# A hybrid attention and recurrence layer: input split and gate products of the recurrence, order of the keys, figures of the scheduler

## The chip, the cores and the metric

The kernel runs on one NeuronCore of a Trainium2 chip. The metric is the device time of one execution in microseconds; several runs are given by their median. A trace of one further execution was taken by the hardware profiler.

The engines are called TensorE (PE in the rows; PEld is its weight load), VectorE (DVE), ScalarE (ACT), GpSimd (POOL) and SyncE (SP), which issues the DMAs. PSUM, which TensorE writes, has eight banks of 128 partitions by 512 fp32.

## The reference

One encoder layer runs over two sequences, a prompt of 512 tokens and a sample of 1024, both of width 1024 in fp32, with the same weights. The parts that matter here:

```python
n = rms_norm(x, ln1_g) * (1 + sc1) + sh1           # sh, sc, g come from silu(c) @ w_ada
q, k, v, xl, gl = split(n @ w_in)                  # 512 columns each
q, k = rms_norm per head (8 heads of 64)
att = neighbourhood_attention(q, k, v, rpb)        # grid rows of 64 tokens, window of 8 x 16 keys, softmax
xl = depthwise_conv(xl, lru_conv_w, lru_conv_b)    # width 4
for each direction (forward, backward):
    r = sigmoid(blockwise xl @ w_r + b_r)          # 8 blocks of 64 x 64
    i = sigmoid(blockwise xl @ w_i + b_i)
    a = exp(-8 * r * softplus(-lam)); u = sqrt(1 - a*a) * (i * xl)
    h = scan(h = a*h + u)
lru = (h_forward + h_backward) * gelu(gl)
x = x + g1 * (concat(att, lru) @ w_out)
up = depthwise_conv(n2 @ w_up, ...)                # width 3, 2 x 2816 columns
x = x + g2 * ((gelu(up_1) * up_2) @ w_down)
```

## The kernel before

**Matmuls.** Every fp32 product is made of three: an operand is split into a high part (rounded to the type fp32r) and a low part (the rest), and high x high, high x low and low x high are added in PSUM. `split` (line 493) makes the parts: a copy to fp32r, on ScalarE or VectorE, and a subtraction, on VectorE or GpSimd. The large products of the up and down projections use Strassen-Winograd terms, sums and differences of blocks that are split in their turn.

**Stages**, in order of time: modulation vectors and the first norm (to about 44 us); per column block of 128, the projections of queries, keys, values, recurrence input and gate, first for the prompt, then for the sample, woven with the attention of the block before (to about 610 us); output projection and second norm (to about 840 us); up projection, 22 blocks (to about 1440 us); down projection, seven products of 11 pairs of blocks into six banks each (to the end).

**Recurrence, `lru` (line 1005).** After the convolution, `xc` holds 128 channels, two heads of 64, over all tokens of the sequence. Two buffers are made, one for a head: lines 1026 to 1028 split 64 partitions of `xc` so that the high part lies on the head's own partitions and the low part on the other 64. A gate product of 512 tokens and one direction (`mm2_rows`, line 468) is then, for each head, a matmul over all 128 rows, which adds high x high and high x low since the high weights lie on both halves, and one over 64 rows for the low weights. The two 64-row matmuls of the heads lie on different halves of the array's rows. Four sigmoids of 64 partitions empty the two banks.

**Attention, `attend` (line 1070).** A tile has 128 queries and 256 keys (prompt) or 384 (sample): rows of the grid by 32 columns. The scores come from `mm3_rows` (line 451), six matmuls of 64 rows: three pairs, each with one matmul for either head. Their moving operand is read from the keys in the order row, column: runs of 32. VectorE adds the bias and finds the minimum of the negated scores; the exponential (line 1107) reads the tile in order and writes it with four rows innermost, since the values are laid out so; it goes into a second buffer. TensorE transposes the tile, 128 keys at a time, and multiplies it with the values. `qkv` (line 951) stores the keys: line 985 writes the high part out of PSUM, line 986 the low part.

**Order of the work.** The kernel's functions only record operations, with their tiles and an estimated cost. `run` and `_order` (lines 501 and 561) then simulate the five engines once, on the host, and write each engine's instructions in the resulting order; on the chip each engine follows its list. An operation gets a key, the time by which it must be done for its users; of the ready ones the smallest key goes first. Operations other than matmuls that read or write PSUM get `BOOST` ns off their key (line 521). All instructions of the trace therefore carry the line of `_emit` (L359) or `transpose` (L482), and are known by shape and tile.

**Memory.** SBUF is shared between an arena of fp32r tiles (matmul operands, R) and one of fp32 tiles (F). `STEPS` gives the size of R in KB in each stage, out of 216; the rest is F. Pieces (`piece0F`, `piece0R`, ...) change their owner between stages. The sixth entry is that of the down projection, the seventh that of its last product. A tile is placed ahead of its turn only where the memory still suffices for what comes before it.

Of the kernel before, what the change touches and what calls it, by code (L numbers as in the profile page):

```python
# [18 lines left out]
P = 128  # L19
# [12 lines left out]
STEPS = (140, 134, 160, 176, 186, 64, 124)  # L32
# [15 lines left out]
BOOST = 3e5  # L48

LANES = 8  # L50

# [165 lines left out]
class Recorder:  # L217
# [208 lines left out]
    def mm(self, out, lhsT, rhs, start, stop, tile_position=None, also=(), cost=None, go_on=False):  # L426
        n = self._n(rhs)
        if cost is None:
            cost = max(max(64.0, n) / 2.4 + 13.5, 109.0) if rhs.ap.dtype == F32R else max(214.0, n / 0.6)
        kw = dict(out=out, lhsT=lhsT, rhs=rhs, start=start, stop=stop)  # L430
        if tile_position is not None:
            kw["tile_position"] = tile_position
        if go_on:
            kw["skip_group_check"] = True
        w = [out]
        if start:

            w.append(View(out.buf, self._shadow(512, F32), ())[out.span()[0]:out.span()[1], :])
        self.op("PE", cost, self._emit(self.nc.tensor.matmul, kw), [lhsT, rhs], w, also=also)
# [11 lines left out]
    def mm3_rows(self, outs, sts, mvs):  # L451

        n = self._n(mvs[0][0])
        kws = []
        for a, b, start, stop in ((0, 0, True, False), (0, 1, False, False), (1, 0, False, True)):
            for out, st, mv in zip(outs, sts, mvs):
                kws.append(dict(out=out, lhsT=st[a], rhs=mv[b], start=start, stop=stop))
        calls = [self._emit(self.nc.tensor.matmul, kw) for kw in kws]

        def go():  # L460
            for c in calls:
                c()
        w = list(outs)
        for out in outs:
            w.append(View(out.buf, self._shadow(512, F32), ())[out.span()[0]:out.span()[1], :])
        self.op("PE", 3 * (max(64.0, n) / 2.4 + 13.5), go, [v for pr in sts + mvs for v in pr], w)

    def mm2_rows(self, outs, sts, mvs):
# [10 lines left out]
        self.op("PE", 3 * (max(64.0, n) / 2.4 + 13.5), go, [v for pr in sts + mvs for v in pr], list(outs))  # L479
# [21 lines left out]
    def run(self):  # L501
# [5 lines left out]
        for o in ops:  # L507
            if o.eng == "PE":
                vt += o.cost
            o.vt = vt  # L510
            for q in o.deps:
                q.users.append(o)

        for o in reversed(ops):
# [6 lines left out]
            if o.eng != "PE" and not o.strict and any(b.dram is None and b.arena.key == "P" for b in o.bufs):  # L521
                o.key -= BOOST
        base = {}
# [37 lines left out]
    def _order(self, occ):  # L561
# [87 lines left out]
        while count < n:  # L649
# [92 lines left out]
            o.start, o.end = s, s + o.cost  # L742
# [4 lines left out]
            fin = o.end  # L747
# [34 lines left out]
def encoder(ctx: ExitStack, tc: tile.TileContext, x_p, x_s, c_t, ada, bada, bgate, lng, w_qkv, w_xg,  # L782
# [168 lines left out]
    def qkv(q, get, j, out, w, early=False):  # L951
# [3 lines left out]
        for g in range(halves):  # L955
# [29 lines left out]
            R.act(kh[:, c0:c0 + 512], pk, AF.Copy, scale=qkgt[:, 1:2])  # L985
            R.stt(kl[:, c0:c0 + 512], pk, qkgt[:, 1:2], kh[:, c0:c0 + 512].bitcast(F32), ALU.mult, ALU.subtract)
# [18 lines left out]
    def lru(q, get, c, wxg=None, early=False):  # L1005
# [17 lines left out]

        xs = [R.buf([P, nT], F32R, "xcs") for _ in range(2)]
        half = (slice(0, 64), slice(64, P))
        for hd in range(2):
            a, b = half[hd], half[1 - hd]
            R.split(xs[hd][a], xs[hd][b], xc[a])
# [4 lines left out]
        for d in range(2):  # L1033
            for b in blk:
                pg = [R.bank("gate") for _ in range(2)]
                R.mm2_rows(pg, [(gh[:, hd, d, :], gl[half[hd], hd, d, :]) for hd in range(2)], [(x[:, b], x[a, b]) for x, a in zip(xs, half)])
# [33 lines left out]
    def attend(q, j, kqs):  # L1070
# [16 lines left out]
        for grp in groups:  # L1087
            vs = {cb: values(cb) for cb in sorted({cb for _, cb in grp})}
            po = [R.bank("po").rearrange("p (u h d) -> p u h d", u=2, h=2) for _ in range(2)]
            for u, (half, cb) in enumerate(grp):  # L1090
# [5 lines left out]
                for hh in range(2):  # L1096
                    hp = slice(64 * hh, 64 * hh + 64)
                    pS.append(R.bank("S")[:, 0:nk])
                    mvs.append([t[hp, :].rearrange("p (r c) -> p r c", c=64)[:, r0:r0 + nr, KB[cb]:KB[cb] + 32] for t in (kh, kl)])
                    sts.append([x[hp, cb * P:cb * P + P] for x in qs[half]])  # L1100
                R.mm3_rows(pS, sts, mvs)
                for hh in range(2):
                    e, mn, sm, ri = R.buf([P, nk], F32, "e"), small(1, "mn"), small(1, "sm"), small(1, "ri")
                    R.vec("tensor_tensor_reduce", e, [pS[hh], bi[:, hh, :]], in0=pS[hh], in1=bi[:, hh, :], scale=-1.0, scalar=3e38, op0=ALU.add, op1=ALU.min, accum_out=mn)

                    e, raw = R.buf([P, nk], F32, "e"), e
                    R.act(e.rearrange("p (a c r) -> p a r c", c=32, r=4), raw.rearrange("p (a r c) -> p a r c", r=4, c=32), AF.Exp, scale=-1.0, bias=mn, accum_out=sm)
# [467 lines left out]
def _places():  # L1575
# [3 lines left out]
    for rows, halves, knr in ((8, 1, 8), (16, 2, 12)):  # L1579
# [12 lines left out]
        out.append(at.reshape(halves * 4, P, knr * 32))  # L1592
# [72 lines left out]
```

## Time and profile before

| | |
|---|---|
| Runs | 1752.65, 1755.28, 1757.9 us; median 1755.28 us |
| Profiled execution | 1756.22 us, of it the span 1754.4 us |
| TensorE busy | 1683.2 us (96%), 8882 matmuls |
| VectorE busy | 1330.6 us (76%) |
| ScalarE busy | 844.6 us (48%) |
| GpSimd busy | 567.4 us (32%) |
| Mean granted TensorE clock | 0.978 of 2.4 GHz |

The busy time of an engine is the union of its instructions; matmuls overlap, so the mean duration of one says less than the distance between starts. The clock that is granted to TensorE has two levels, 1.2 and 2.4 GHz (0.5 and 1.0 in the rows); a number between is a mean over a stretch.

### The profile page before, as it was taken

What the parts mean: (1) busy time and instruction counts of PE and PEld (TensorE: products, weight loads), DVE (VectorE), ACT (ScalarE), POOL (GpSimd) and SP (SyncE); (2) the same over time, 40 slices, a digit from 0 to 9 for tenths busy, and PEclk for the clock granted to TensorE, in tenths of its full rate; (3) what the DMA queues carried; (4) which work ended last, traced back from release to release, by engine and by line L of the source; (5) the groups of instructions that cost most, each with busy time, mean ns of one, the idle gap of its engine ahead of it and who ended that gap; (6) DMA issues with size and microseconds to landing.
All of it is one profiled execution on the core that took longest, in us unless ns stands there. A gap on an engine that the chain in (4) does not pass through costs nothing. (4 is left out here: it accounts for less than half of the span.)

```text
span 1754.4 us, 24769 instructions
## 1 busy us (share of the span) xinstructions
PE 1683.2 (96%) x8882; PEld 1399.7 (80%) x8882; DVE 1330.6 (76%) x2467; ACT 844.6 (48%) x1444; POOL 567.4 (32%) x353
## 2 busy tenths in 40 slices
PE   6999989999999799998999999999999999998998
PEld 3777687978696588897888888888888787886887
DVE  4788885887878875877777676767677867899785
ACT  3478963868585942364444343434345521232331
POOL 0023130030201210535332222222223402899993
PEclk9999989999999899999999999999999999998999
DMA  9654442252516574552121212121212468577661
GB/s 345 228 180 142 153 137 90 94 204 67 207 52 238 177 243 147 178 195 67 43 85 57 70 57 70 57 71 57 71 62 90 141 236 291 195 274 225 221 213 60
DMA packets 130476, 253.88 MB, mean 145 GB/s; under 512 B 13600, under 2 KB 45984, under 8 KB 130352
## 3 DMA queue, kind: packets, MB, share of 16 engines
q1 hardware_dynamic: 130352, 252.29, 42.5%
q8 instruction: 70, 1.15, 0.3%
q14 instruction: 54, 0.44, 0.1%
HBM read 207.66 MB, written 44.58 MB: 144 GB/s over the span
## 5 line engine op out<-in xcount | busy, mean ns | idle before, releaser
L359 PE MATMUL bank<-arena_r 128*128 128x512 f32 (+2 forms) x2224 | 498.3, 361 | 16.0 <-DVE piece0F L359 7.6
L359 PEld LDWEIGHTS bank<-arena_r 128*128 128x128 f32 (+1 forms) x2224 | 390.2, 192 | 84.4 <-DVE piece0F L359 8.0
L359 PE MATMUL bank<-piece0R,arena_r 128*128 128x512 f32 (+2 forms) x1283 | 353.7, 390 | 1.6 <-DVE arena_s L359 1.6
L359 PE MATMUL bank<-arena_r,piece0R 128*128 128x384 f32 (+3 forms) x1549 | 325.9, 336 | 1.7 <-DVE piece0R L359 1.2
L359 PEld LDWEIGHTS bank<-arena_r,piece0R 128*128 128x128 f32 (+1 forms) x1549 | 254.5, 189 | 28.3 <-issue 12.3
L359 PEld LDWEIGHTS bank<-piece0R,arena_r 128*128 128x128 f32 (+1 forms) x1283 | 230.0, 190 | 57.7 <-issue 12.4
L359 POOL TENSOR_TENSOR arena_f<-arena_f 128x512 f32<-128x512 f32 (+2 forms) x87 | 128.0, 1471 | 354.3 <-DMA arena_f<-in_w_up_dram 157.9
L359 POOL TENSOR_TENSOR arena_r<-arena_f,arena_r 128x512 fp32r<-128x512 f32 (+2 forms) x62 | 97.9, 1583 | 285.0 <-ACT arena_r L359 157.6
L359 ACT ACTIVATE arena_f<-arena_f,arena_s 128x384 f32<-128x384 f32 (+2 forms) x196 | 140.9, 768 | 94.9 <-DVE arena_f L359 76.6
L359 DVE SCALAR_TENSOR_TENSOR arena_f<-bank,arena_s,arena_f 128x255 f32<-128x255 f32 (+2 forms) x308 | 155.9, 536 | 30.8 <-ACT arena_f L359 24.0
L359 PE MATMUL bank<-piece0R 128*128 128x512 f32 (+4 forms) x554 | 143.0, 384 | 4.1 <-ACT piece3F L359 2.7
L359 ACT ACTIVATE arena_r<-arena_f 128x512 fp32r<-128x512 f32 (+3 forms) x114 | 78.6, 702 | 120.2 <-PE bank L359 89.6
L359 ACT ACTIVATE arena_f<-bank 128x512 f32<-128x512 f32 (+2 forms) x149 | 70.2, 472 | 124.6 <-DVE bank L359 76.6
L359 DVE TENSOR_TENSOR arena_r<-arena_f,arena_r 128x512 fp32r<-128x512 f32 (+3 forms) x114 | 113.6, 999 | 13.8 <-ACT arena_r L359 8.9
L359 ACT ACTIVATE arena_f<-bank,arena_s 128x512 f32<-128x512 f32 (+1 forms) x133 | 90.7, 687 | 58.3 <-PE bank L359 50.9
L359 PEld LDWEIGHTS bank<-piece0R 128*128 128x128 f32 (+1 forms) x554 | 93.2, 188 | 27.2 <-issue 5.7
L359 DVE TENSOR_TENSOR arena_f<-arena_f 128x512 f32<-128x512 f32 (+1 forms) x76 | 61.3, 810 | 25.9 <-ACT arena_f L359 23.9
L482 PE MATMUL bank<-ident,arena_f 128*128 128x128 f32 x360 | 64.5, 294 | 13.9 <-ACT arena_f L359 9.7
L359 PE MATMUL bank<-piece1R,arena_r 128*128 128x512 f32 (+1 forms) x254 | 75.2, 368 | 0.0
L359 ACT ACT_TABLE_LOAD x51 | 65.4, 1283 | 11.3 <-issue 4.2
L359 PE MATMUL bank<-piece3R,arena_r 128*128 128x256 f32 (+1 forms) x356 | 69.3, 299 | 1.3 <-ACT arena_f L359 1.2
L359 ACT ACTIVATE piece4F<-bank,arena_s 64x512 f32<-64x512 f32 (+1 forms) x68 | 47.4, 704 | 46.3 <-PE bank L482 19.0
(457 smaller groups left out, 2980.6 us busy)
## 6 DMA issues: line engine op xcount, KB each, us to landing
arena_f<-in_w_up_dram SPq DMA_DIRECT2D x100, 256.0 KB, 3.2
arena_f<-gd SPq DMA_DIRECT2D x47, 384.0 KB, 4.1
gd<-arena_f SPq DMA_DIRECT2D x63, 256.0 KB, 3.3
arena_f<-in_bias_s_dram SPq DMA_DIRECT2D x32, 384.0 KB, 4.5
piece4F<-in_ada_dram SPq DMA_DIRECT2D x21, 512.0 KB, 7.5
arena_f<-in_w_qkv_dram SPq DMA_DIRECT2D x28, 384.0 KB, 5.9
piece3F<-in_ada_dram SPq DMA_DIRECT2D x19, 512.0 KB, 6.0
piece0F<-gd SPq DMA_DIRECT2D x21, 384.0 KB, 5.3
```

The costliest lines, as they stand in the source:

```text
L359: fn(**{k: (v.real() if isinstance(v, View) else v) for k, v in kw.items()})
L482: self.op("PE", 107.0, lambda: self.nc.tensor.transpose(out.real(), in_.real(), ident.real()), [in_, ident], [out])
```

## The change

The input of the recurrence is split once per 512 tokens on all 128 partitions into a high and a low buffer. A gate product is made by `mm3_rows`, three pairs of 64-row matmuls. The keys are stored with four rows innermost; the score matmuls read them in runs of 128, the bias is laid out in the same order on the host, and the exponential writes in place, in order. In the planner: `BOOST` falls from 300,000 to 20,000 ns; each key gets a random part of up to 500 ns either way, from a fixed seed; each instruction is charged a further 6 (VectorE), 14 (ScalarE) or 25 ns (GpSimd); half-row groups are charged 100 ns more; plain fp32 matmuls get a delay to their result of 1.2 ns a column; and R has 96 KB instead of 64 in the down projection.

```diff
-STEPS = (140, 134, 160, 176, 186, 64, 124)
+STEPS = (140, 134, 160, 176, 186, 96, 124)
...
-BOOST = 3e5
+BOOST = 2e4
+NOISE, SEED = 500.0, 7
...
+WAITS = {"PE": 0.0, "ACT": 14.0, "DVE": 6.0, "POOL": 25.0, "DMA": 0.0}
...
-        self.op("PE", cost, self._emit(self.nc.tensor.matmul, kw), [lhsT, rhs], w, also=also)
+        self.op("PE", cost, self._emit(self.nc.tensor.matmul, kw), [lhsT, rhs], w, also=also, lat=0.0 if rhs.ap.dtype == F32R else n * 1.2)
...
-        self.op("PE", 3 * (max(64.0, n) / 2.4 + 13.5), go, [v for pr in sts + mvs for v in pr], w)
+        self.op("PE", 3 * (max(64.0, n) / 2.4 + 13.5) + 100.0, go, [v for pr in sts + mvs for v in pr], w)
...
+            if NOISE and not o.strict:
+                o.key += RNG.uniform(-NOISE, NOISE)
...
-            o.start, o.end = s, s + o.cost
+            o.start, o.end = s, s + o.cost + WAITS[e]
...
-            fin = o.end
+            fin = o.end + (o.lat if e == "PE" else 0.0)
...
-            R.act(kh[:, c0:c0 + 512], pk, AF.Copy, scale=qkgt[:, 1:2])
-            R.stt(kl[:, c0:c0 + 512], pk, qkgt[:, 1:2], kh[:, c0:c0 + 512].bitcast(F32), ALU.mult, ALU.subtract)
+            R.act(kh[:, c0:c0 + 512].rearrange("p (a c r) -> p a c r", a=2, r=4), pk.rearrange("p (a r c) -> p a c r", a=2, r=4), AF.Copy, scale=qkgt[:, 1:2])
+            for a in range(2):
+                h, l = (x[:, c0 + 256 * a:c0 + 256 * a + 256].rearrange("p (c r) -> p c r", r=4) for x in (kh, kl))
+                R.stt(l, pk[:, 256 * a:256 * a + 256].rearrange("p (r c) -> p c r", r=4), qkgt[:, 1:2], h.bitcast(F32), ALU.mult, ALU.subtract)
...
-        xs = [R.buf([P, nT], F32R, "xcs") for _ in range(2)]
+        xh, xl = R.pair([P, nT], "xcs")
         half = (slice(0, 64), slice(64, P))
-        for hd in range(2):
-            a, b = half[hd], half[1 - hd]
-            R.split(xs[hd][a], xs[hd][b], xc[a])
+        for b in blk:
+            R.split(xh[:, b], xl[:, b], xc[:, b])
...
-                R.mm2_rows(pg, [(gh[:, hd, d, :], gl[half[hd], hd, d, :]) for hd in range(2)], [(x[:, b], x[a, b]) for x, a in zip(xs, half)])
+                R.mm3_rows(pg, [(gh[a, hd, d, :], gl[a, hd, d, :]) for hd, a in enumerate(half)], [(xh[a, b], xl[a, b]) for a in half])
...
-                    mvs.append([t[hp, :].rearrange("p (r c) -> p r c", c=64)[:, r0:r0 + nr, KB[cb]:KB[cb] + 32] for t in (kh, kl)])
+                    mvs.append([t[hp, :].rearrange("p (a x) -> p a x", x=256)[:, half:half + nch, 4 * KB[cb]:4 * KB[cb] + P] for t in (kh, kl)])
...
-                    e, raw = R.buf([P, nk], F32, "e"), e
-                    R.act(e.rearrange("p (a c r) -> p a r c", c=32, r=4), raw.rearrange("p (a r c) -> p a r c", r=4, c=32), AF.Exp, scale=-1.0, bias=mn, accum_out=sm)
+                    R.act(e, e, AF.Exp, scale=-1.0, bias=mn, accum_out=sm)
...
-        out.append(at.reshape(halves * 4, P, knr * 32))
+        out.append(at.reshape(halves * 4, P, knr // 4, 4, 32).swapaxes(3, 4).reshape(halves * 4, P, knr * 32))
```

## Rows read from the trace of the kernel before

**Rows 1.** The page, engines: busy us, share of the span, instructions.
```profile
PE 1683.2 (96%) x8882; PEld 1399.7 (80%) x8882; DVE 1330.6 (76%) x2467; ACT 844.6 (48%) x1444; POOL 567.4 (32%) x353
```
**Rows 2.** Windows, seven stages: length, busy us by engine, clock, DMA share, GB/s.
```profile
0.00:44.00 44.00, 30.44 (x143) 15.29 (x145) 21.80 (x77) 15.29 (x23) 0.96 (x7) 0.92 0.90 346
...
200.00:310.00 110.00, 98.86 (x524) 81.43 (x523) 82.91 (x227) 69.03 (x121) 19.16 (x13) 0.92 0.29 97
...
570.00:614.00 44.00, 31.30 (x154) 22.91 (x155) 38.07 (x84) 42.21 (x70) 12.76 (x5) 0.81 0.51 178
...
760.00:840.00 80.00, 71.27 (x473) 66.23 (x473) 60.41 (x81) 39.03 (x66) 40.13 (x26) 0.91 0.29 86
840.00:1320.00 480.00, 479.98 (x2757) 423.29 (x2756) 346.68 (x643) 194.23 (x343) 121.77 (x89) 1.00 0.21 66
...
1480.00:1625.00 145.00, 134.33 (x573) 109.87 (x572) 134.53 (x92) 38.67 (x54) 131.26 (x69) 0.95 0.71 241
...
1710.00:1754.40 44.40, 38.87 (x171) 31.52 (x169) 23.20 (x31) 5.35 (x8) 15.20 (x7) 0.98 0.16 60
```
**Rows 3.** Windows, sum over the eight half-clock stretches after 200 us.
```profile
sum 68.10, PE 47.70 PEld 37.95 DVE 58.58 ACT 44.50 POOL 27.40; mean PE 5.96 PEld 4.74 DVE 7.32 ACT 5.56 POOL 3.43
```
**Rows 4.** Timeline 570 to 594, ScalarE and TensorE: start, us, instruction, idle before.
```profile
580.70 0.68 ACT L359 ACTIVATE piece3F<-bank,arena_s 64x512 f32<-64x512 f32 x1
...
584.49 1.28 ACT L359 ACT_TABLE_LOAD   x1
...
585.78 0.99 ACT L359 ACTIVATE arena_f<-arena_f,arena_s 128x384 f32<-128x384 f32 x1
...
589.16 1.54 PE L482 MATMUL bank<-ident,arena_f 128*128 128x128 f32 x6 [6.27 <-ACT arena_f L359]
...
591.13 0.61 ACT L359 ACTIVATE arena_f<-arena_f,arena_s 128x384 f32<-128x384 f32 x1
```
**Rows 5.** Timelines of TensorE and of VectorE, 1594 to 1622.
```profile
1594.68 15.80 PE L359 MATMUL bank<-arena_r 128*128 128x512 f32 x69
1618.08 4.21 PE L359 MATMUL bank<-arena_r 128*128 128x512 f32 x9 [7.60 <-DVE piece0F L359]
...
1614.55 2.28 DVE L359 TENSOR_TENSOR piece4F<-piece4F,piece0F 128x512 f32<-128x512 f32 x1
1616.75 0.68 DVE L359 TENSOR_TENSOR piece0F<-bank,piece5F 128x512 f32<-128x512 f32 x1
```
**Rows 6.** Timeline of TensorE, 295 to 309: gate groups and one score tile.
```profile
295.71 0.73 PE L359 MATMUL bank<-arena_r,piece0R 128*128 128x512 f32 x2
296.38 0.49 PE L359 MATMUL bank<-arena_r 64*128 64x512 f32 x2
296.80 0.73 PE L359 MATMUL bank<-arena_r,piece0R 128*128 128x512 f32 x2
...
304.32 0.63 PE L359 MATMUL bank<-arena_r,piece0R 128*128 128x512 f32 x2
304.88 0.51 PE L359 MATMUL bank<-arena_r 64*128 64x512 f32 x2
305.32 0.38 PE L359 MATMUL bank<-piece1R,piece2R 128*128 128x256 f32 x1
...
307.72 0.80 PE L359 MATMUL bank<-arena_r,piece0R 64*128 64x384 f32 x6
308.45 0.44 PE L359 MATMUL bank<-arena_r,piece1R 128*128 128x384 f32 x1
```
**Rows 7.** Lines by form, VectorE, 44 to 616: count, busy us, mean ns, idle.
```profile
L359 DVE TENSOR_TENSOR piece0R<-piece4F,piece0R 128x512 fp32r<-128x512 f32 x5 | 3.4, 689 | 0.2 <-ACT piece0R L359 0.2
...
L359 DVE TENSOR_TENSOR arena_r<-piece4F,arena_r 64x1024 fp32r<-64x1024 f32 x2 | 2.4, 1220 | 0.1
```
**Rows 8.** Lines by form, ScalarE, 570 to 614.
```profile
L359 ACT ACTIVATION_READ_ACCUMULATOR arena_f<-arena_f,arena_s 128x1 f32 x11 | 2.3, 209 | 0.0
```
**Rows 9.** The page, DMA issues: count, size, median us to landing.
```profile
arena_f<-gd SPq DMA_DIRECT2D x47, 384.0 KB, 4.1
```

More of the change, by code (lines that the diff above doesn't have):

```diff
@@ L1 @@
 import heapq
+import random
 from contextlib import ExitStack
@@ L478, in go @@
                 c()
-        self.op("PE", 3 * (max(64.0, n) / 2.4 + 13.5), go, [v for pr in sts + mvs for v in pr], list(outs))
+        self.op("PE", 3 * (max(64.0, n) / 2.4 + 13.5) + 100.0, go, [v for pr in sts + mvs for v in pr], list(outs))
     def transpose(self, out, in_, ident):
@@ L512, in run @@
                 q.users.append(o)
+        RNG = random.Random(SEED)
         for o in reversed(ops):
```

## The prediction

> **What bounds the kernel now.** I read the page's engine table first, then busy time by stage, then the granted clock beside it, then the timeline of the stretches where TensorE stands idle. In the engine table TensorE is busy 1683.2 us of 1754.4 [rows 1]; the reader should take from it that only 71.2 us of the span are not matrix work, so the change can earn from three things alone: this idle time, the slow clock that follows it, and fewer or better packed matmuls. The stage table says where the idle time lies [rows 2]. In the first 44 us 13.6 us are idle (loads in a strict order, which the diff leaves alone), and 5.5 us at the end; between lie 52 us, of which 11.1 (200 to 310 us, call it A), 12.7 (570 to 614, E), 8.7 (760 to 840, F) and 10.7 (1480 to 1625, J) make 43. From 840 to 1320 us TensorE is never idle, and nothing can be won there. The same rows show the granted clock below 1.0 in A, E, F and J, and at both ends. The eight stretches after 200 us at 1.2 GHz last 68.1 us and hold 47.7 us of busy TensorE [rows 3]; at 2.4 GHz that work takes half, so the slow clock costs 23.9 us. Spread over the 52 us of idle time, one idle microsecond costs 1.46. Priced so, A is 16 us, E 18.5, F 12.7, J 15.6, and the ceiling of any better order is 52 + 24 = 76 us.
>
> Why E is idle is seen on ScalarE, which is busy 42.2 of 44 us there [rows 2]. The last of a row of 64-partition sigmoids ends at 581.4, then come other functions with a table load each, the second at 584.49 for 1.28 us, and the first exponential starts only at 585.78; TensorE's transposes have waited 6.27 us for it when they start at 589.16 [rows 4]. The sigmoids read PSUM, and the planner puts everything that touches PSUM 300 us ahead of its due time. In J TensorE ends its matmuls at 1610.5 (1594.68 + 15.80) and starts again at 1618.08, 7.60 us later, on a VectorE sum that empties a bank; VectorE came to the first of these sums at 1616.75, after a 128x512 sum of 2.28 us, while the sum out of PSUM takes 0.68 [rows 5]. VectorE (134.5 of 145 us) and GpSimd (131.3) are nearly full in that stage [rows 2].
>
> **The change part by part.**
>
> *Gate products.* There are 24 groups (4 column blocks, 2 directions, 1 + 2 token blocks). Before, a group is two 128-row matmuls and one pair on half the rows; after, three such pairs. Pairs do run side by side: the six 64-row matmuls of a score tile take 0.73 us to the next start, and three matmuls of that width, one after the other, would take 3 x 0.229 x 384/512 = 0.515 (a step of 512 columns is 15.80 / 69 = 0.229), so each pair costs about one matmul, and 0.21 goes to entering and leaving the half-row form; the matmul ahead pays another 0.10 (two 128x512 before a pair take 0.56 where two steps are 0.46) [rows 5, 6]. A group after is thus 3 x 0.229 + 0.31 = 1.00 us; a group before, standing alone, takes 304.32 to 305.32, also 1.00. Alone it gains nothing. Standing in a chain, a group before takes 1.09 (295.71 to 296.80) because it changes form twice [rows 6], while after it needs only its three pairs, 0.69. In the timeline 9 of the 24 groups follow another directly: 9 x 0.40 = 3.6 us. Bounds: 0 (none chained) and 9.6 us (all). I take 4.
>
> *Input split.* Before, each column block takes two high and two low halves on 64 partitions over all tokens; after, one each per 512 tokens on 128. A low half of 64x1024 costs VectorE 1.22 us, one of 128x512 0.69 [rows 7]. For the long sequence 4 x 2 x 1.22 = 9.8 becomes 4 x 2 x 0.69 = 5.5; the short one goes from 8 to 4 of 0.69, 2.8 us less. About 7 us leave VectorE or GpSimd, and as much again at the price of ScalarE or VectorE copies. No row lets TensorE wait for these for over a microsecond, so by themselves they are worth 0 to 2 us; I count them inside A and E.
>
> *Keys.* The exponential of a 128x384 tile with its permuted write costs 0.99 us, a plain ScalarE pass of that shape with a scale vector 0.61 [rows 4]: 0.38 us less for 64 tiles is 24 us, and with two thirds of that for the 32 tiles of 256 columns, 8 us more: some 32 us of ScalarE, all ahead of 616 us. The permutation moves to 12 key stores, which now read PSUM at steps of 256 bytes: one ScalarE pass of 512 each, and on VectorE one pass of 512 becomes two of 256. No row shows such a read. Bounds: below, nothing but the second instruction's start (under 0.3 us each); above, the 0.38 per 384 that the permuted write paid, 0.5 us a pass, 6 us on each engine. I take 3, hidden, since keys are stored a whole column block ahead of their use. The score matmuls read 128 keys in one run instead of four runs of 32; before, their pairs already step at the rate of whole matmuls (above), so 0.
>
> The Trainium skill, page "SBUF — State Buffer", section on Door 1 with its note on cachelines, says that every access that crosses to a new 16-byte line of SBUF pays a penalty, and that PSUM's lines are 8 bytes, so that patterns with gaps there slow matmuls. The first half fits the 0.99 against 0.61 (a 16-byte step in the old write). The second, carried over from matmuls to the key store, speaks against this edit: the cost would come back there. By it ScalarE's gain would be 32 less 6 and VectorE would lose 6, the upper bound above; the sum would stay, since both stand beside TensorE.
>
> *The planner.* Nothing of it runs on the chip, but every queue is ordered anew. It now charges 100 ns more for a half-row group (0.31 measured above), a tail for fp32 matmuls, and 6, 14 and 25 ns more per instruction on VectorE, ScalarE and GpSimd; it takes the lead of PSUM readers down from 300 to 20 us, and adds up to 0.5 us of chance to each key. So the order is better informed, and it is also another draw. My shares of the stalls' prices: E: eleven exponentials run there, each with a read of its sum behind it [rows 8] (11 x 0.38 = 4.2 us of ScalarE), and they are no longer behind every sigmoid: half, -9. A: ScalarE too, but with only 256-wide tiles and norms: a third, -5. F: none of its work changes, only its order: a quarter, -3. J: below, half, -7. What is late next in E is ScalarE's own work, still some 37 of 44 us (42.2 less 4.2 and a share of the splits), which is why I take no more. The bounds for each: all of it gone, or as much again.
>
> *Memory of the last stage.* The matmul operands' arena there grows from 64 to 96 KB, the rest shrinks from 152 to 120. The terms of one pair of blocks take 10 KB (768 and 512 columns, high and low), so 9 pairs instead of 6 can be ready; a pair feeds TensorE 18 x 0.229 = 4.1 us, so the lead grows from 25 to 37 us, over the 7.60 us of J. Against it: kept sums and differences (55 KB), partial outputs (36) and gate rows (8) leave 21 KB for loads in flight instead of 53, two pairs instead of five.
>
> **Sum.** -4 -9 -5 -3 -7 = -28 us. Against the profiled execution's own 1756.2 us (1.8 outside the span) that is 1728; the median of the runs shown is 0.9 lower, so 1727.
>
> **Rivals.**
>
> *The stalls only move.* The new order has gaps elsewhere of the same price: ScalarE's long run of sigmoids and table loads stays. For it: 30 of the 43 idle microseconds of the four places are in A, F and J, whose work the diff hardly touches. Against: E and A are ScalarE's and that is where 32 us leave. Only the gates' 4 us remain: 1751 give or take 8.
>
> *The last stage starves (slower).* With 21 KB for loads, two pairs are in flight. A load of 384 KB lands after 4.1 us in the median [rows 9], a sum beside GpSimd takes 2.3 [rows 5] and I count a split as much: some 10 us in transit, 5 us a pair against the 4.1 that TensorE takes. Over the three products that need sums (33 pairs) that is 0.9 x 33 = 30 us, and 14 for the clock at 0.46 each. J's gain is lost: 1727 + 7 + 44 = 1778. It decides as soon as a pair's transit passes 8.2 us while the lead of 9 pairs is used up. Against it: buffers of the first two products are not yet filled by sums, and the lead covers 37 us.
>
> *Most of the stalls go.* If E and J vanish and A and F halve: 4 + 18.5 + 15.6 + 8 + 6 = 52 us, 1703. For it: each of the four has one late instruction behind it; against: four independent pieces of luck.
>
> *The pairs do not run side by side at 512 columns.* Then each of the 24 groups costs 3 x 0.229 more, 16 us: 1747 with the 4 lost. The score tiles say otherwise [rows 6].
>
> **How the numbers follow.** The forecast has 0.55 (its own range 1708 to 1748), stalls that only move 0.19, starving 0.10, most stalls gone 0.12, no side-by-side 0.04. A measurement of this kernel tells 0.3%, 5.3 us, from no change: the bounds are 1750 and 1760.5. Faster: 0.55 + 0.12 + 0.04 and 0.05 of the moved stalls, 0.76. Within: 0.09. Slower: 0.05 of the moved stalls and the starving, 0.15. The range 1700 to 1766 leaves out half of the best case, most of the starving and little else, under 0.2.
>
> **What will show it.** Right: exponentials of 128x384 near 0.61 us; the 64x1024 splits gone; gate groups as six 64-row matmuls, 0.69 us apart where chained; fewer than 68 us at 1.2 GHz after 200 us; no idle stretch of 7 us at a product's end in the last stage; 840 to 1320 us still full. Wrong: idle time in the stage that was full, for the smaller lead of PSUM readers; GpSimd and VectorE waiting for loads after 1480 us; or the same idle sum at other places.

## The result: 1773.3 us, slower than before by 1.0%

| | before | after |
|---|---|---|
| Median beside each other, 4 runs each | 1756.1 us | 1773.3 us |
| Ratio, with its 95% interval | | 1.0104 (1.0091 to 1.0116) |
| Span of the profiled execution | 1754.4 us | 1769.7 us |
| TensorE busy | 1683.2 us | 1676.7 us |
| TensorE idle | 71.2 us | 93.0 us |

The forecast of 1727 and its range, 1700 to 1766, both missed. The page of the kernel after, engine table, answers to [rows 1]:

```profile
PE 1676.7 (95%) x8930; PEld 1402.8 (79%) x8930; DVE 1351.4 (76%) x2499; ACT 834.3 (47%) x1431; POOL 547.8 (31%) x341
```

TensorE works 6.5 us less and stands idle 21.8 us more: that is the 15.3 us of span. Busy time by stage of the kernel after, columns as in [rows 2]. The last two stretches are counted back from the end of the span, as far from it as J (1480 to 1625) and the 85 us behind J were before, since the work there ends 15.3 us later:

```profile
200.00:310.00 110.00, 97.99 (x556) 86.24 (x553) 80.33 (x207) 62.15 (x119) 24.17 (x17) 0.92 0.29 95
310.00:437.00 127.00, 106.93 (x588) 88.51 (x588) 85.24 (x211) 84.12 (x139) 9.84 (x6) 0.91 0.30 103
437.00:525.00 88.00, 83.12 (x490) 69.79 (x489) 70.29 (x169) 67.74 (x127) 17.78 (x12) 1.00 0.45 149
525.00:760.00 235.00, 223.18 (x1112) 180.85 (x1112) 181.34 (x343) 117.66 (x216) 47.73 (x25) 0.96 0.56 187
760.00:840.00 80.00, 73.12 (x549) 70.01 (x548) 61.95 (x91) 46.88 (x77) 40.33 (x26) 0.98 0.44 144
840.00:1320.00 480.00, 472.83 (x2686) 414.44 (x2685) 357.80 (x651) 179.54 (x307) 102.20 (x74) 1.00 0.20 62
840.00:1495.30 655.30, 644.82 (x3488) 557.25 (x3487) 496.33 (x857) 251.36 (x423) 161.00 (x113) 1.00 0.28 90
1495.30:1640.30 145.00, 139.72 (x604) 114.32 (x603) 120.35 (x95) 40.94 (x57) 118.67 (x63) 0.98 0.71 240
1640.30:1725.30 85.00, 82.46 (x363) 67.34 (x362) 78.51 (x62) 30.32 (x43) 71.61 (x41) 1.00 0.66 227
```

The same stages of the kernel before, where [rows 2] has none:

```profile
310.00:437.00 127.00, 125.25 (x737) 107.84 (x736) 102.38 (x253) 98.21 (x175) 19.78 (x12) 1.00 0.35 120
437.00:525.00 88.00, 86.74 (x463) 68.60 (x464) 67.90 (x162) 62.10 (x109) 13.99 (x8) 0.96 0.39 134
525.00:760.00 235.00, 218.81 (x1118) 176.39 (x1118) 175.88 (x333) 122.57 (x211) 51.35 (x27) 0.96 0.60 203
840.00:1480.00 640.00, 637.97 (x3469) 553.34 (x3468) 465.15 (x820) 254.54 (x438) 166.05 (x119) 1.00 0.29 94
1625.00:1710.00 85.00, 85.00 (x377) 70.38 (x376) 69.47 (x56) 29.79 (x44) 78.73 (x46) 1.00 0.66 218
```

The length less the first busy time is TensorE's idle time (J is 1480 to 1625 before and 1495.3 to 1640.3 after):

| us of idle TensorE | before | after | |
|---|---|---|---|
| 200 to 310 (A) | 11.1 | 12.0 | +0.9 |
| 310 to 525 | 3.0 | 24.9 | +21.9 |
| 525 to 760 (E and its surroundings) | 16.2 | 11.8 | -4.4 |
| 760 to 840 (F) | 8.7 | 6.9 | -1.8 |
| 840 to J | 2.0 | 10.5 | +8.5 |
| J and the 85 us behind it | 10.7 | 7.8 | -2.9 |

The four places that the prediction priced won 8.2 us together. The stages that had been full, or nearly so, lost 30.4: that is the result. With 0.4 us less idle time outside these stages it makes the 21.8. (E is taken with its surroundings because its last wait of 3.27 us now falls at 636 us.)

The slow clock changed little. The sum over the half-clock stretches after 200 us, which answers to [rows 3], is 72.7 us with 51.1 busy, against 68.1 with 47.7: the 3.4 us more of busy time there cost 1.7 us, since at 2.4 GHz that work takes half.

```profile
sum 72.70, PE 51.11 PEld 45.36 DVE 59.73 ACT 41.82 POOL 15.77; mean PE 4.26 PEld 3.78 DVE 4.98 ACT 3.48 POOL 1.31
```

The largest new hole, in the timeline of the kernel after, TensorE, VectorE and ScalarE's table loads; columns as in [rows 4]:

```profile
353.72 3.27 PE L363 MATMUL bank<-arena_r 128*128 128x384 f32 x13
...
355.53 1.28 ACT L363 ACT_TABLE_LOAD   x1
...
357.37 2.28 DVE L363 TENSOR_TENSOR_SCAN piece3F<-piece5F,piece4F 128x1024 f32<-128x1024 f32 x1
...
357.89 1.28 ACT L363 ACT_TABLE_LOAD   x1
...
360.36 1.23 DVE L363 SCALAR_TENSOR_TENSOR piece4F<-piece3F,piece4F 128x1024 f32<-128x1024 f32 x1 [0.72 <-ACT piece3F L363]
...
362.10 1.22 DVE L363 TENSOR_TENSOR piece4F<-piece4F,piece3F 128x1024 f32<-128x1024 f32 x1
...
363.31 0.29 DVE L363 TENSOR_TENSOR arena_r<-bank,arena_r 128x128 fp32r<-128x128 f32 x1
...
363.51 2.28 DVE L363 TENSOR_TENSOR_SCAN piece3F<-piece3F,piece4F 128x1024 f32<-128x1024 f32 x1
...
363.65 1.01 PE L363 MATMUL bank<-arena_r,piece0R 64*128 64x384 f32 x4 [6.67 <-DVE arena_r L363]
...
371.59 2.82 PE L486 MATMUL bank<-ident,arena_f 128*128 128x128 f32 x12 [6.61 <-DVE arena_f L363]
```

From 356 to 372 us VectorE and ScalarE work through one column block's recurrence, passes of 1.2 to 2.3 us, most functions of ScalarE behind a table load. In between stands an emptying of PSUM that takes 0.29 us, and TensorE waits 6.67 us for it; then 6.61 us more for the attention tile behind the second scan. Before, all of 310 to 437 was idle for 1.8 us, where 20.1 stand now.

In the last stage J's one hole of 7.60 us ([rows 5]), which ended 136 us before the end, has become four smaller ones, 142 to 127 us before the end. Timeline of TensorE in the kernel after:

```profile
1599.68 26.68 PE L363 MATMUL bank<-arena_r 128*128 128x512 f32 x117
1627.59 1.65 PE L363 MATMUL bank<-arena_r 128*128 128x512 f32 x6 [1.23 <-POOL arena_r L363]
1631.77 2.64 PE L363 MATMUL bank<-arena_r 128*128 128x512 f32 x6 [2.52 <-POOL arena_r L363]
1635.93 5.09 PE L363 MATMUL bank<-arena_r 128*128 128x512 f32 x15 [1.53 <-POOL arena_r L363]
1642.52 2.85 PE L363 MATMUL bank<-arena_r 128*128 128x512 f32 x11 [1.50 <-DVE piece1F L363]
```

GpSimd is not waiting for loads in these microseconds; its splits stand end to end in its timeline:

```profile
1627.50 2.54 POOL L363 TENSOR_TENSOR arena_r<-arena_f,arena_r 128x768 fp32r<-128x768 f32 x1
1630.00 1.71 POOL L363 TENSOR_TENSOR arena_r<-piece4F,arena_r 128x512 fp32r<-128x512 f32 x1
1631.67 2.54 POOL L363 TENSOR_TENSOR arena_r<-arena_f,arena_r 128x768 fp32r<-128x768 f32 x1
1634.16 1.72 POOL L363 TENSOR_TENSOR arena_r<-piece0F,arena_r 128x512 fp32r<-128x512 f32 x1
```

Loads do come late for other engines. In the last 274 us of the span ScalarE waits 14.1 us for loads in all, against 0.6 before, and VectorE 3.1 against 0.2; GpSimd waits 19.5 against 21.0. The longest of ScalarE's sums in the kernel after, from its waits from 1495 us on (us in total, times, longest):

```profile
ACT arena_r L363 <- DMA arena_f<-gd: 6.7, 4, 3.0
```

The local edits did what was written of them. Two gate groups in a chain, TensorE of the kernel after:

```profile
113.31 0.34 PE L363 MATMUL bank<-arena_r,piece1R 128*128 128x384 f32 x1
113.58 0.50 PE L363 MATMUL bank<-piece2R,piece0R 64*128 64x512 f32 x2
113.92 0.40 PE L363 MATMUL bank<-piece0R 64*128 64x512 f32 x2
114.15 0.63 PE L363 MATMUL bank<-piece2R,piece0R 64*128 64x512 f32 x4
114.61 0.39 PE L363 MATMUL bank<-piece0R 64*128 64x512 f32 x2
114.84 0.40 PE L363 MATMUL bank<-piece2R,piece0R 64*128 64x512 f32 x2
115.17 0.62 PE L363 MATMUL bank<-arena_r,piece2R 128*128 128x384 f32 x2
```

Twelve matmuls of 64 rows take 1.59 us (113.58 to 115.17). Pairs start 0.23 us apart, so a group behind another takes 3 x 0.23 = 0.69, the forecast figure, against 1.09 in [rows 6]. In TensorE's list of the kernel after, 9 of the 24 groups follow another directly, as many as the prediction counted.

### The profile page after: what moved, and what is told of

Its sections match the earlier page's. It is cut to its first block, busy times and chain, and to the rows that moved or that the text cites. A ratio compares the mean times of both kernels' runs of the same rounds, so it can differ in the third digit from the quotient of the medians.

```text
span 1769.7 us, 24912 instructions
## 1 busy us (share of the span) xinstructions
PE 1676.7 (95%) x8930; PEld 1402.8 (79%) x8930; DVE 1351.4 (76%) x2499; ACT 834.3 (47%) x1431; POOL 547.8 (31%) x341
## 4 chain that ended last, share of the span: by engine, by line
PE 82%; DVE 9%; ACT 4%; DMA 2%; issue 1%; POOL 1%; SPq 0%; ACTq 0%; DVEq 0%; POOLq 0%
PE bank L363 78%; DVE arena_f L363 3%; PE bank L486 3%; DVE arena_r L363 2%; DVE piece3F L363 1%; ACT piece3F L363 1%; POOL arena_r L363 1%; ACT arena_f L363 1%; DVE piece4F L363 1%; ACT L363 1%; DVE arena_s L363 1%; DMA arena_f<-in_w_up_dram 1%; DMA arena_f<-in_w_down_dram 1%; ACT piece4F L363 0%; SPq L363 0%
## 5 line engine op out<-in xcount | busy, mean ns | idle before, releaser
L363 PE MATMUL bank<-arena_r 128*128 128x512 f32 (+3 forms) x2880 | 700.2, 368 | 22.6 <-DVE arena_r L363 7.8
L363 PEld LDWEIGHTS bank<-arena_r 128*128 128x128 f32 (+1 forms) x2880 | 517.5, 191 | 114.7 <-DVE arena_r L363 11.9
L363 PE MATMUL bank<-arena_r,piece5R 128*128 128x256 f32 (+1 forms) x1211 | 283.4, 332 | 4.5 <-DVE piece5R L363 4.4
L363 PEld LDWEIGHTS bank<-arena_r,piece5R 128*128 128x128 f32 x1211 | 204.3, 190 | 29.8 <-DVE piece5R L363 4.8
L363 PE MATMUL bank<-arena_r,piece0R 128*128 128x384 f32 (+3 forms) x838 | 208.5, 360 | 6.7 <-DVE arena_r L363 6.7
L363 PE MATMUL bank<-piece0R,arena_r 128*128 128x512 f32 (+4 forms) x589 | 179.4, 388 | 1.5 <-ACT arena_f L363 0.6
L363 POOL TENSOR_TENSOR arena_r<-arena_f,arena_r 128x768 fp32r<-128x768 f32 (+2 forms) x63 | 109.4, 1748 | 228.3 <-DMA arena_f<-in_w_qkv_dram 110.9
L363 DVE SCALAR_TENSOR_TENSOR arena_f<-bank,arena_s,arena_f 128x255 f32<-128x255 f32 (+3 forms) x308 | 156.0, 536 | 25.1 <-ACT arena_f L363 18.8
L363 PEld LDWEIGHTS bank<-arena_r,piece0R 128*128 128x128 f32 (+1 forms) x838 | 145.8, 191 | 21.1 <-DVE arena_r L363 7.8
L363 PEld LDWEIGHTS bank<-piece0R,arena_r 128*128 128x128 f32 (+1 forms) x589 | 103.4, 189 | 33.4 <-issue 13.0
L486 PE MATMUL bank<-ident,arena_f 128*128 128x128 f32 x336 | 60.8, 295 | 18.1 <-DVE arena_f L363 10.7
```

The source lines that it names most:

```text
L363: fn(**{k: (v.real() if isinstance(v, View) else v) for k, v in kw.items()})
L486: self.op("PE", 107.0, lambda: self.nc.tensor.transpose(out.real(), in_.real(), ident.real()), [in_, ident], [out])
```

## The experiments

All times are medians beside runs of the kernel before on the same chip, which gave 1755.8 to 1756.9. The theories: the random part of the keys makes another order, and its worth is luck (D, the draw); the shorter lead of PSUM readers makes the holes (P); the corrected costs do (W); the edits themselves do; random keys do harm whatever the seed (N).

**One planner figure at a time, and the edits alone.**

```diff
# a_boost300: after
-BOOST = 2e4
+BOOST = 3e5
# a_nonoise: after
-NOISE, SEED = 500.0, 7
+NOISE, SEED = 0.0, 7
# a_seed8: after
-NOISE, SEED = 500.0, 7
+NOISE, SEED = 500.0, 8
# edits_only: the edits of lru, qkv, attend and the bias; all planner figures and STEPS of before, no random part
```

Expected of a_boost300: 

> The changed kernel with the lead of PSUM readers back at 300 us (BOOST 3e5), all else as changed. Theory P (the cut lead lets recurrence work on VectorE and ScalarE go ahead of small instructions that empty PSUM, and TensorE waits): the two idle stretches of 6.7 and 6.6 us at 357 to 372 go, TensorE's idle time from 310 to 437 us falls from 20 us to under 6, and the time falls from 1773 to 1720 to 1750. Theory D (any new order is a draw; the lead has no part of its own): 1773 give or take 12, with as much idle time in the stages of the prompt and the sample, only at other places. Theory W (the planner's corrected figures are what misleads it): no change beyond D, since they stay.

Expected of a_nonoise: 

> The changed kernel without the random part of the keys (NOISE 0). Theory P: the lead stays cut, so the time stays within 12 us of 1773, and idle time from 310 to 437 us stays above 10 us. Theory D: it is another draw, anywhere from 1740 to 1790. A fall below 1745 would say that the random keys alone did the harm.

Expected of a_seed8: 

> The changed kernel with another seed (8 instead of 7) for the random part of the keys. It sizes the draw. Theory P: within 12 us of 1773, with more than 10 us idle from 310 to 437 us. Theory D: anywhere from 1740 to 1790, the place of the long gaps unlike that of seed 7.

Expected of edits_only: 

> The edits of the kernel alone (input split, gate pairs, order of the keys), with every figure of the planner as before (lead 300 us, no random part, no extra charges, 64 KB in the last stage). Theory P: faster than before, 1735 to 1752, with ScalarE some 30 us less busy and chained gate groups 0.69 us apart. Theory D: 1756 give or take 15. If it is as slow as the changed kernel (above 1768), the edits and not the planner's figures are the cause.

| run | us | ratio, 95% | idle | idle 310 to 525 |
|---|---|---|---|---|
| a_boost300 | 1763.9 | 1.0054 (1.0024 to 1.0083) | 86.1 | 11.5 |
| a_nonoise | 1737.3 | 0.9896 (0.9867 to 0.9925) | 73.5 | 11.7 |
| a_seed8 | 1758.3 | 1.0014 (0.9994 to 1.0033) | 75.6 | 5.4 |
| edits_only | 1755.8 | 0.9997 (0.9986 to 1.0009) | 74.8 | 0.7 |

Without the random part the changed kernel is 36 us faster; another seed alone takes 15 off and all but empties 310 to 525. Windows of a_nonoise, columns as in [rows 2]:

```profile
310.00:437.00 127.00, 119.66 (x713) 100.44 (x713) 105.31 (x277) 93.46 (x190) 25.88 (x17) 0.97 0.44 151
...
840.00:1320.00 480.00, 480.00 (x2759) 423.69 (x2758) 340.14 (x644) 189.34 (x333) 119.68 (x87) 1.00 0.22 66
```

The stage 840 to 1320 is full again with the lead still at 20 us, so a short lead need not make a hole there; edits_only has 4.6 us idle in it with the long lead. With the lead restored and seed 7 kept, 9 us come back: a quarter of what the random part is worth. Of the 36 us some 20 are idle time; 5 more are the clock (41 us of busy half clock after 200 us against 51), and 11 are busy time of TensorE. Of these 11, 9 lie in the 192 matmuls with 32 stationary columns that make the modulation vectors: from start to next start they take 42.7 us in one order and 33.6 in the other. The edits alone, in an order made with the old figures, give the time of before (1755.8 against 1755.9, interval 0.14% less to 0.09% more).

**How far a draw goes, and P and the memory without it.** Seeds 9 and 4 were the best and worst of twelve in the planner's own reckoning.

```diff
# a_seed9, a_seed4: after, SEED 9 or 4
# a_nonoise_boost300: a_nonoise
-BOOST = 2e4
+BOOST = 3e5
# a_nonoise_steps64: a_nonoise
-STEPS = (140, 134, 160, 176, 186, 96, 124)
+STEPS = (140, 134, 160, 176, 186, 64, 124)
```

Expected of a_seed9: 

> The changed kernel with seed 9. So far the same kernel took 1773 with seed 7, 1758 with seed 8 and 1737 without the random part. Theory D (the random keys draw an order, and the draw outweighs every other part of the planner's change): the order for this seed ends earliest of those that the planner's own run on the host gave for twelve seeds, so below 1740, the fastest so far. Theory P (the cut lead of PSUM readers sets the time): the lead is the cut one, so the two idle stretches of over 6 us in the sample's attention should come back, 1755 or more. Theory N (random keys harm by themselves, since they break the order of equally urgent work): 1755 or more, like seeds 7 and 8.

Expected of a_seed4: 

> The changed kernel with seed 4, for which the planner's own run on the host ends latest of twelve seeds. Theory D: slower than seed 7, 1790 to 1820, the idle time in some stage that seeds 7 and 8 keep busy. Theories P and N: like seeds 7 and 8, 1755 to 1775.

Expected of a_nonoise_boost300: 

> The changed kernel without random keys (1737) and with the lead of PSUM readers back at 300 us. Theory P: faster than 1737, 1715 to 1733. Theory D: anywhere in 1737 give or take 18; slower than 1745 would say that the smaller lead is not what harms, and that the 9 us between seed 7 at 20 us and seed 7 at 300 us came from the draw.

Expected of a_nonoise_steps64: 

> The changed kernel without random keys and with the last stage's operand memory back at 64 KB. The forecast's account of that stage (more operands ready ahead cover the product's end): the idle time after the up projection rises from 13 to 20 us or more and the stretch of some 7 us at a product's end comes back, so 1737 + 7 to 15 = 1744 to 1752. Theory S (the last stage starves on 96 KB): faster than 1737. The stages before 800 us should keep their order, since the figure touches the last stage; if they change much, the draw enters here too.

| run | us | ratio, 95% | idle |
|---|---|---|---|
| a_seed9 | 1730.4 | 0.985 (0.9822 to 0.9879) | 58.6 |
| a_seed4 | 1811.0 | 1.0309 (1.0279 to 1.0339) | 112.5 |
| a_nonoise_boost300 | 1743.0 | 0.9922 (0.9893 to 0.9951) | 71.4 |
| a_nonoise_steps64 | 1754.0 | 0.9989 (0.9973 to 1.0004) | 82.5 |

Seeds 9 and 4 came where D had them, and one integer moves the time by 81 us. In a_seed4 the hole of the kernel after stands at the same place, larger; its timeline, VectorE and TensorE:

```profile
354.98 1.22 DVE L363 TENSOR_TENSOR piece4F<-piece4F,piece3F 128x1024 f32<-128x1024 f32 x1 [1.76 <-ACT piece4F L363]
358.62 1.23 DVE L363 SCALAR_TENSOR_TENSOR piece3F<-piece5F,piece3F 128x1024 f32<-128x1024 f32 x1 [2.41 <-ACT piece5F L363]
...
366.31 2.29 DVE L363 TENSOR_TENSOR_SCAN piece4F<-piece4F 128x1024 f32<-128x1024 f32 x1
...
371.76 0.55 DVE L363 CUSTOM_DVE_ANT_0 arena_f<-bank,arena_f 128x384 f32<-128x384 f32 x1
...
374.86 0.90 PE L486 MATMUL bank<-ident,arena_f 128*128 128x128 f32 x3 [19.07 <-DVE arena_f L363]
```

The attention's minimum (0.55 us) waits behind the whole recurrence, and TensorE behind it for 19.07 us. In a_seed9 nothing of the kind is left; its windows:

```profile
310.00:525.00 215.00, 212.29 (x1253) 180.53 (x1250) 168.79 (x439) 157.14 (x301) 35.11 (x22) 0.99 0.39 132
525.00:900.00 375.00, 356.28 (x1996) 303.36 (x1995) 292.40 (x496) 183.17 (x319) 113.29 (x72) 0.97 0.48 158
...
1455.70:1685.70 230.00, 228.51 (x1007) 188.61 (x1006) 189.52 (x149) 72.82 (x103) 197.00 (x109) 1.00 0.73 250
```

The lead has no sign of its own: restoring it gives 9 us with seed 7 and costs 6 without random keys. With 64 KB, 17 us are lost; but TensorE's order in that run differs from a_nonoise's from 50 us on, long before the last stage, so the 17 hold a new draw as well. The stretch of some 7 us at a product's end, which was expected to come back, did not: the longest in that stage is 5.87 us.

**A cost with the order held, and figures one by one.**

```diff
# a_seed9_expstride: a_seed9; every engine's list is otherwise the same
-                    R.act(e, e, AF.Exp, scale=-1.0, bias=mn, accum_out=sm)
+                    ep = e.rearrange("p (a c r) -> p a r c", c=32, r=4)
+                    R.act(ep, ep, AF.Exp, scale=-1.0, bias=mn, accum_out=sm)
# b_noise7: before, with the random part of the keys, seed 7
# a_nonoise_nofig: a_nonoise, without WAITS, the 100 ns and the matmul's delay
# b_boost20: before
-BOOST = 3e5
+BOOST = 2e4
```

Expected of a_seed9_expstride: 

> Seed 9 (1730), with the exponential still in place but read and written in the permuted order with a 16-byte step; every engine's list of instructions is the same as with seed 9, so nothing is drawn anew. The result of the kernel is the same. It sets the price of the 96 slow exponentials (32 us of ScalarE) with the order held. Theory H (ScalarE's gain is hidden beside TensorE): 1730 to 1734. Theory E (ScalarE sets the pace in the sample's attention, as the forecast had it for a part): 1736 to 1745. All on the path: 1762.

Expected of b_noise7: 

> The kernel before with one thing added: the random part of up to 500 ns on each key, seed 7, its lead of 300 us and all other figures kept. Theory D: the order is drawn anew and leaves 1756 by 10 us or more; the planner's own run on the host ends later than without the random part, so slower, 1766 to 1780. Theory K (the slowdown belongs to the kernel's edits or the cut lead): within 5 us of 1756.

Expected of a_nonoise_nofig: 

> The changed kernel without random keys (1737) and without the planner's corrected costs (no charge per instruction, no 100 ns for half-row groups, no tail of fp32 matmuls); lead 20 us and 96 KB stay. Theory W (the corrected costs mislead): faster than 1730. Theory C (they help): 1745 or more, with more idle time of under 2 us each in the attention. Theory D: another draw, 1737 give or take 18, which would leave W and C open.

Expected of b_boost20: 

> The kernel before with the lead of PSUM readers cut from 300 to 20 us and nothing else. Theory P: slower, 1770 to 1790, by idle stretches behind recurrence work on VectorE as in the changed kernel at 357 to 372 us. Theory D: a draw, 1745 to 1790; faster than 1750 would end theory P.

| run | us | ratio, 95% | idle |
|---|---|---|---|
| a_seed9_expstride | 1741.5 | 0.9914 (0.9883 to 0.9945) | 63.3 |
| b_noise7 | 1781.9 | 1.0144 (1.0115 to 1.0174) | 88.7 |
| a_nonoise_nofig | 1746.3 | 0.9938 (0.9915 to 0.996) | 73.1 |
| b_boost20 | 1769.9 | 1.0076 (1.0046 to 1.0105) | 80.4 |

The first is the only clean price of an edit. ScalarE by form, a_seed9 and then a_seed9_expstride (count, busy us, mean ns, idle):

```profile
L363 ACT ACTIVATE arena_f<-arena_f,arena_s 128x384 f32<-128x384 f32 x95 | 57.0, 610 | 16.4 <-DVE arena_s L363 16.3
...
L363 ACT ACTIVATE arena_f<-arena_f,arena_s 128x256 f32<-128x256 f32 x65 | 33.9, 528 | 28.5 <-DVE arena_f L363 23.0 <-DVE arena_s L363 5.4
```

```profile
L363 ACT ACTIVATE arena_f<-arena_f,arena_s 128x384 f32<-128x384 f32 x95 | 81.4, 869 | 12.2 <-DVE arena_s L363 12.0
...
L363 ACT ACTIVATE arena_f<-arena_f,arena_s 128x256 f32<-128x256 f32 x65 | 41.8, 655 | 27.3 <-DVE arena_f L363 23.1 <-DVE arena_s L363 4.2
```

The stepped exponentials cost ScalarE 24.4 + 7.9 = 32 us, as the prediction counted, and the kernel 11 (two runs each: 1729.0 and 1731.9 against 1739.3 and 1743.7), as theory E had it. Since the lists are the same, the two traces also tell where. Windows to the same matmul of TensorE's list, at the end of the attention, in a_seed9 and then in a_seed9_expstride (one more is counted, since it reaches over the edge):

```profile
0.00:623.52 623.52, 583.12 (x3242) 461.10 (x3243) 483.50 (x1264) 414.28 (x773) 113.28 (x79) 0.98 0.48 166
0.00:636.29 636.29, 592.09 (x3243) 464.58 (x3243) 486.42 (x1265) 443.67 (x773) 112.91 (x79) 0.97 0.47 164
```

The stepped one is 12.8 us behind there. Counted at the same matmuls it was 4.0 behind when a_seed9 stood at 200 us, 6.6 at 310 and 9.6 at 525, so the loss comes in all of the attention, little by little; 3 us of it are won back by 840.

The random part alone makes the kernel before 25 us slower, and a shorter lead alone 13, which is most of the 17 that the whole change cost; at the lower edge of P's range; but TensorE is idle for only 2.0 us from 310 to 437 in b_boost20, so the stretches that P named did not come. Leaving out the corrected costs loses 9 us, within a draw: open.

**More draws of both kernels**, seeds not chosen by any reckoning.

```diff
# a_seed1, a_seed2, a_seed3, a_seed5: after, SEED 1, 2, 3, 5
# b_noise1, b_noise3: as b_noise7, seeds 1 and 3
```

Expected of a_seed1: 

> The changed kernel with seed 1, one of four seeds taken in order and not by any rank. If seed 7 was only unlucky, the middle of the four lies below 1750 and is clear of the kernel before; if random keys cost time on the whole, against 1737 without them, it lies at 1755 or above. The planner's own run ranks this one first of the four: 1735 to 1755.

Expected of a_seed2: 

> The changed kernel with seed 2, one of the same four. The planner's own run ranks it last of the four, near seed 8 (1758): 1755 to 1768.

Expected of a_seed3: 

> The changed kernel with seed 3, one of the same four. The planner's own run ranks it second, close to seed 1: 1735 to 1755.

Expected of a_seed5: 

> The changed kernel with seed 5, one of the same four. The planner's own run ranks it third, beside seed 8: 1750 to 1765.

Expected of b_noise1: 

> The kernel before with random keys of up to 500 ns and seed 1, nothing else. If the order of the kernel before is better than its own draws (1756 without the random part, 1782 with seed 7), slower than 1765; if seed 7 was unlucky for it too, 1745 to 1765.

Expected of b_noise3: 

> The kernel before with random keys of up to 500 ns and seed 3, nothing else. The planner's own run on the host ends earlier for it than for seeds 1 and 7. If the order of the kernel before is better than its own draws: 1762 to 1775; otherwise 1745 to 1758.

| order | after | before |
|---|---|---|
| no random part | 1737.3 | 1756 |
| seed 1 | 1748.6 (0.9921 to 0.9966) | 1814.7 (1.0303 to 1.0363) |
| seed 2 | 1756.8 (0.9984 to 1.0015) | |
| seed 3 | 1749.0 (0.9923 to 0.9975) | 1776.2 (1.0084 to 1.0143) |
| seed 5 | 1752.4 (0.9954 to 0.9981) | |
| seed 7 | 1773.3 (1.0091 to 1.0116) | 1781.9 (1.0144 to 1.0174) |
| seed 8 | 1758.3 (0.9994 to 1.0033) | |
| middle of the seeds | 1754.6 | 1781.9 |

(Intervals are of the ratio.) Seed 7 is the slowest of the six of after. Before's own order is 20 to 58 us faster than its three draws, so an unlucky draw was compared with an order better than draws. After, too, is faster without the random part than with any of the six seeds, by 17 us at their middle: of seed 7's 36 us, 17 are what random keys cost in the middle and 19 are its own bad luck. Only seed 9, chosen as the best of twelve, beats the order without. So random keys need not harm (N as stated fell with a_seed9), but in ten of eleven draws they did. The four seeds taken in order have their middle at 1750.7, between the two outcomes named for them. Like against like the change is faster: 1737 against 1756 without a random part, 19 us, each of the two a single order; by the middles 27. With three and six draws so far apart, 27 is rough.

The draws were not blind. The expectations above, written before the runs, hold the ranks that the planner's own run on the host gave: seed 9 first and 4 last of twelve, then 1, 3, 5 and 2, with 8 beside 5 and 2; for the kernel before, seed 3 ahead of 1 and 7. The chip kept all these ranks, up to differences within the intervals. Where a time was forecast from them, b_noise7 and b_noise3 came 2 and 1 us above their ranges.

All these orders together also tell what the edits did in two stages, as far as draws let it be seen. TensorE's idle time from 525 to 900 us was 24.9 to 37.3 in five orders with the stepped exponentials (before, b_boost20, b_noise1, 3 and 7; middle 28.5), and 18.4 to 38.8 in fourteen with the plain ones (middle 25). In J and the 85 us behind it, it was 7.4 to 17.2 us in seven orders with 64 KB (before, b_boost20, the three b_noise, edits_only, a_nonoise_steps64; middle 11.4), and 1.5 to 14.5 in twelve with 96 KB (middle 7.8; a_seed9_expstride, which has the list of a_seed9, is left out of both counts). Both lean the way of the forecast, by some 3.5 us each; both ranges overlap.

## Why the prediction was wrong

**The failed step** is the planner's, in its sentences "So the order is better informed, and it is also another draw. My shares of the stalls' prices". The draw got no term. Shares were taken for four places that stood idle, gains all; the places that stood full, which a new order can only lose, had none. At the prediction's own 1.46 a microsecond, the 24 us forecast there are 16 of idle time; 8.2 came. The full stages took 30.4, for which the sum had nothing. "Another draw" is worth 36 us here (a_nonoise against after), and 81 from one seed to another. The price itself was no constant either: 21.8 us more of idle time came with 1.7 us of slow clock here, 1.1 for each, while a_seed4, with 19.6 us more idle time than the kernel after and 84 us of busy half clock after 200 us against 51, pays 16.5 us of slow clock on top, 1.8 for each.

**The rivals.** "The stalls only move" named the mechanism, but assumed that the sum stays; it was the nearest, and its 1751 give or take 8 did not reach 1773. "The last stage starves" was right in that loads land later for their users with 96 KB, and wrong in what follows from it: the waits are there (ScalarE's 14.1 us of waits above; in the last 274 us 2.3 to 46.5 in the twelve orders with 96 KB, 0 to 8.2 in the seven with 64), but TensorE's idle time there shrank from 10.7 to 7.8 us, and the waits that are left to it are for splits that GpSimd runs end to end and for one VectorE sum. That its 1778 is close to the result is chance. The side-by-side rival fell by the chained groups. Of the signs of being wrong the first came (idle time in 840 to 1320), but its cause as put there, the smaller lead, did not hold: a_nonoise has that lead and no idle microsecond in that stage. The second came in part: VectorE waits for loads after 1480 us where it hardly did, GpSimd no more than before.

**Right in their places.** Gate groups came as forecast, 0.69 us apart in a chain, nine of them chained; what they are worth in the sum can't be read off, since TensorE's busy time differs by 11 us between two orders of the same work. Exponentials: ScalarE's 128x384 passes fell from a mean of 835 ns, stepped ones among them, to 608; the 64x1024 splits are gone, and no stretch of 7 us is left at a product's end. Fewer than 68 us at 1.2 GHz did not come (72.7). With the order held the plain exponentials are worth 11 us, where the prediction gave E and A, ScalarE's two places, 9 and 5: the size was near, the place was not. At the same matmuls the stepped run loses 2.6 us in A and 2.8 in E; the other 7 of the 12.8 come from 44 to 200 us and from 310 to 560, where the forecast had nothing to win.

**The key store.** The reordered ScalarE pass out of PSUM, 128x512, takes 685 ns (by form, after) and took 686 before; VectorE takes 474 to 478 ns for 256 columns at a step, and 478 for the same instruction on 256 columns in order. The upper bound of 0.5 us a pass was not met anywhere: a step of 256 bytes costs neither engine anything, and VectorE pays only for two instructions in place of one (2 x 475 against 749 ns, 0.2 us). The Trainium skill, "SBUF — State Buffer", section on Door 1, says that an access which crosses to a new 16-byte line pays a penalty; the trace agrees for the stepped SBUF write (32 us over 96 passes above). What the page says of PSUM is about matmuls, and carrying it over to these two engines was wrong.

**Settled and open.** Shown: the random part of seed 7 makes the kernel 36 us slower, and the lead, the only other figure changed alone with seed 7 kept, gives 9 back. Argued from timelines only: that the worst holes come when a column block's recurrence runs in one piece on VectorE and ScalarE ahead of short PSUM work (two orders show it, at 356 to 375 us). Open: the separate worth of the corrected costs, the lead and the 96 KB, each of which also draws a new order; which early choice decides that a draw is bad; why random keys cost time in the middle; and whether the planner's own run, which ranked the seeds rightly, would have put the change behind the kernel before.

The experiments also leave two orders that beat both kernels, a_seed9 at 1730.4 and a_nonoise at 1737.3.

## What to carry to other kernels

Where a host program orders the instructions, any change to a cost, a size or a key is also a new draw; measure several draws of both versions first, and take their spread (here 25 us over six seeds, 81 with the best and worst) into the range. Where the planner ends with a time of its own, use it to rank the draws: here it ranked every seed for which its rank is on record as the chip did. To price an edit, hold every engine's list and change the instruction alone. Look at the full stages too: there a new order can win nothing and may lose.

## What was not expected of the hardware

A permuted PSUM read at a step of 256 bytes is free on ScalarE (685 against 686 ns for 128x512), while a write into SBUF at a step of 16 bytes costs the same engine 0.38 us for 128x384 (24.4 us over the 64 stepped passes; the means of 610 and 869 ns above are over stepped ones and others). In a_seed9_expstride the read steps too; in the kernel before only the write did, and a pass took 0.99 us all the same [rows 4], which is 610 ns and the 0.38. And 32 us of added work on ScalarE, busy 825 of 1730 us, cost 11 us of time: an engine at 48% still sets the pace in places.
